# Transposes deferred behind the next scores in a hybrid attention trunk, and one key tile written in place of copied

## The chip, the cores and the metric

One core of a Trainium2 chip runs the whole program. The metric is the device time of one execution in microseconds (us), the median of several; lower is better. The engines that matter here are PE (TensorE, matmuls and transposes), DVE (VectorE), ACT (ScalarE), POOL (GpSimd) and the DMA queues.

## What is computed

Two layers over x (512 tokens, 1024 wide, float32). Each layer normalizes x, projects it with one matrix of 4096 columns, runs two groups of attention heads on the result, gates both, and projects back:

```python
h = rmsnorm(x, norm_g[l]);  proj = h @ w_in[l]
out_a = neighborhood_attention(q_a, k_a, v_a, na_rpb[l])        # group A: 8 heads x 64
p = softmax(q_b k_b^T / 8 + t5_bias)                            # group B: 4 heads, two maps each
out_b = rmsnorm((p[:, 0] - lam * p[:, 1]) @ v_b, subln_g[l]) * (1 - lam_init)
y = concat([out_a * silu(g_a), out_b * silu(g_b)]);  x = x + y @ w_out[l]
```

A last RMSNorm closes the trunk.

## The kernel before

Every float32 matmul is made of three (or two) passes on operands that are split into a high and a low part: ACT casts the value to the high part, DVE subtracts that from the value and writes the low part. `split` (L178) does this for a PSUM tile.

Each layer's projection is cut into 16 units of 256 columns (`ORDER`, L32): VB/VA are values, QB/QA queries and keys, GB/GA gates. A unit is a stream of single matmuls: `proj_fm` (L225) yields a 24-pass group of 512 columns, `proj_tm` (L239) a 24-pass group of 256. The generator `flow` (L578) strings the units together, and `fill(ns)` (L580) pulls matmuls worth `ns` nominal nanoseconds out of it (230 for a wide one, 118 for a narrow one). So projection matmuls are poured, as filling, between the steps of attention. When a 24-pass group is complete its evacuation is issued at that very place in the program: `evac_q` and `evac_k` (two pairs of an ACT cast and a DVE subtraction each), `evac_gate` (ACT tanh, DVE `u`), or `split` for values. `W.piece()` (L129) issues one piece of the weight splitting (`hi` on ACT, L116; `lo` on DVE, L121).

No scheduler reorders any of this: `pinned` chains every engine's instructions in the order in which the Python code issues them. Each engine therefore works off its own fixed list.

Group B (`attn_b`, L290) has 4 tiles of 128 queries per head. A tile: 4 score matmuls (L344); per map a DVE bias-and-minimum (L347) and an ACT exponential (L350); DVE reciprocal, ACT scaling (L356), DVE combination `e` (L358); some 26 filling matmuls; then 4 transposes of `e` on PE (L369) and their `split` (`pth` on ACT L179, `ptl` on DVE L180). After tile 1 and tile 3 a pair is complete, and `weigh` (12 matmuls with the values, L300) is put on the list `late`, which the next tile runs 1400 nominal ns behind its scores. After the second pair `close` prepares the head's norm, and `head_norm` goes on the list `later`: a matmul, DVE `row` (L320), three small POOL steps with DMAs between them, and POOL's product with `rb` (L329). `rb` and the gate's `u` (L280) share two buffers.

Group A (`attn_a`, L375) has the same shape with 8 heads as its steps: 8 score matmuls (L386), 4 minimum/exponential steps, a normalization, some 35 filling matmuls, 8 transposes (L414), and `weigh` (8 matmuls into the one `pv` bank, L421) in the next head.

`evac_k` (L263) writes keys into partitions 0 to 63 of `kt` and then has a DMA (L273) copy them to partitions 64 to 127, since the score matmul needs them twice. At each layer's start the scores of head 0 wait for QB0's keys.

Of the kernel before, what the change touches and what calls it, by code (L numbers as in the profile page):

```python
# [9 lines left out]
F32 = mybir.dt.float32  # L10
# [21 lines left out]
ORDER = ("VB0", "QB0", "QB1", "VB1", "QB2", "GB0", "QB3", "VA0", "QA0", "GB1",  # L32
         "QA1", "VA1", "QA2", "QA3", "GA0", "GA1")
FILL_B = 5400
FILL_A = 7800
A_TILES = ((0, 1), (1, 1), (2, 1), (0, 3))
A_PV = ((1, 128, 128, 0, 128), (3, 640, 256, 256, 128), (0, 0, 768, 0, 384), (2, 384, 128, 128, 128))
NA_BLOCKS = ((0, (0, 1, 2, 3)), (1, (0, 1, 2, 3)), (3, (2, 3, 0, 1)))
# [9 lines left out]
def hybrid_encoder(ctx: ExitStack, tc: tile.TileContext, x, norm_g, w_in, na_rpb,  # L48
# [211 lines left out]
            res.append(q)  # L260
        return res

    def evac_k(pp, natural):  # L263
        kt = qk.tile([P, 4, S], F32R, name="kt", bufs=2)
        for m in range(2):
            src = pp[64 * m:64 * m + 64, :]
            kh, kl = kt[0:64, m, :], kt[0:64, 2 + m, :]
            if natural:
                src = src.rearrange("p (b r c) -> p b r c", r=ROWS, c=C8)
                kh, kl = (z.rearrange("p (r b c) -> p b r c", r=ROWS, c=C8) for z in (kh, kl))  # L270
            A.copy(out=kh, in_=src)
            V.tensor_tensor(out=kl, in0=src, in1=kh.bitcast(F32), op=ALU.subtract)  # L272
        soon.append(lambda: A.dma_start(out=kt[64:128].bitcast(F32), in_=kt[0:64].bitcast(F32)))  # L273
        return [(kt[:, m, :], kt[:, 2 + m, :]) for m in range(2)]

    def evac_gate(pp):
# [3 lines left out]
        V.scalar_tensor_tensor(out=u, in0=th, scalar=1.0, in1=pp, op0=ALU.add, op1=ALU.mult)  # L280
        return u

    late, later = [], []

    def run(jobs):
        while jobs:
            jobs.pop(0)()


    def attn_b(h, q, k, vt, yb, nlam, sg, yout, fill, finished):  # L290
        pair = {}

        def weigh(qp):
            if qp == 0:
                pair["pv"] = ps_v.tile([P, S], F32, name="pv")
            pv, (ph, pl) = pair["pv"], pair[qp]
            n = 0
            for kt in range(4):
                for vs, pp in ((0, ph), (0, pl), (1, ph)):
                    T.matmul(out=pv[:, qp * 256:(qp + 1) * 256], lhsT=vt[:, kt, h % 2, vs, :], rhs=pp[:, kt, :],  # L300
                             start=(n == 0), stop=(n == 11))
                    n += 1
            if qp == 1:
                close(pv)

        def close(pv):
            sq, su = (work.tile([64, S], F32, name=nm, tag="s2", bufs=3) for nm in ("sq", "su"))
            A.activation(out=sq, in_=pv[0:64], func=AF.Square)
            A.activation(out=su, in_=pv[64:P], func=AF.Square)
            V.tensor_tensor(out=sq, in0=sq, in1=su, op=ALU.add)  # L310
            A.activation(out=yout, in_=pv, func=AF.Copy, scale=sg)
            sr = work.tile([P, S], F32R, name="sr", tag="s2", bufs=3)
            A.copy(out=sr[0:64], in_=sq)
            V.tensor_tensor(out=sr[64:P], in0=sq, in1=sr[0:64].bitcast(F32), op=ALU.subtract)
            later.append(lambda: head_norm(pv, sr))

        def head_norm(pv, sr):
            T.matmul(out=pv[0:2, :], lhsT=ones_r, rhs=sr, start=True, stop=True)
            row = work.tile([1, S], F32, name="row", tag="th", bufs=2)
            V.tensor_scalar(out=row, in0=pv[0:1, :], scalar1=1.0 / P, scalar2=1e-5, op0=ALU.mult, op1=ALU.add)  # L320
            ms = small.tile([P, 4], F32, name="ms")
            nc.gpsimd.dma_start(out=ms, in_=row.rearrange("o (p a) -> o p a", a=4))  # L322
            rs = small.tile([P, 4], F32, name="rsb")
            G.tensor_tensor(out=rs, in0=ms, in1=nhalf, op=ALU.pow)
            rs_d = dram.tile([1, S], F32, name="rs_d", bufs=2)
            nc.gpsimd.dma_start(out=rs_d.rearrange("o (p a) -> (o p) a", a=4), in_=rs)
            rb = work.tile([P, S], F32, name="rb", tag="u", bufs=2)
            nc.gpsimd.dma_start(out=rb, in_=rs_d.broadcast_to([P, S]))
            G.tensor_tensor(out=yout, in0=yout, in1=rb, op=ALU.mult)  # L329
            finished()  # L330

        for qt in range(4):
            qp, qi = divmod(qt, 2)
            if qi == 0:
                pair[qp] = [w4.tile([P, 4, 256], F32R, name=nm, tag="w4k") for nm in ("pth", "ptl")]
            e = w4.tile([P, 2, S], F32, name="w4k")
            mn = small.tile([P, 2], F32, name="mn")
            z = small.tile([P, 2], F32, name="z")
            sts = []
            for m in range(2):  # L340
                st = ps_s.tile([P, S], F32, name="st")
                sts.append(st)
                for i in range(2):
                    T.matmul(out=st, lhsT=q[m][:, qt * P:(qt + 1) * P], rhs=k[m][i], start=(i == 0), stop=(i == 1))  # L344
            for m, st in enumerate(sts):
                lt = work.tile([P, S], F32, name="lt", bufs=2)
                V.tensor_tensor_reduce(out=lt, in0=st, in1=yb[:, 48 - 16 * qt:560 - 16 * qt],  # L347
                                       scale=-1.0, scalar=3e38, op0=ALU.add, op1=ALU.min,
                                       accum_out=mn[:, m:m + 1])
                A.activation(out=e[:, m, :].rearrange("p (b r c) -> p b r c", r=ROWS, c=C8),  # L350
                             in_=lt.rearrange("p (r b c) -> p b r c", r=ROWS, c=C8),
                             func=AF.Exp, bias=mn[:, m:m + 1], scale=-1.0, accum_out=z[:, m:m + 1])
            W.piece()
            rz = small.tile([P, 2], F32, name="rz")
            V.reciprocal(out=rz, in_=z)
            A.activation(out=e[:, 0, :], in_=e[:, 0, :], func=AF.Copy, scale=rz[:, 0:1])  # L356
            V.tensor_scalar_mul(rz[:, 1:2], rz[:, 1:2], nlam)
            V.scalar_tensor_tensor(out=e[:, 0, :], in0=e[:, 1, :], scalar=rz[:, 1:2], in1=e[:, 0, :],  # L358
                                   op0=ALU.mult, op1=ALU.add)
            fill(700)  # L360
            run(later)
            W.piece()
            fill(700)
            run(late)
            W.piece()
            fill(FILL_B - 1400)
            pt = ps_t.tile([P, 4, P], F32, name="pt")
            for kt in range(4):
                T.transpose(out=pt[:, kt, :], in_=e[:, 0, kt * P:(kt + 1) * P], identity=ident)  # L369
            split(pt, *(z[:, :, qi * P:(qi + 1) * P] for z in pair[qp]))  # L370
            if qi == 1:
                late.append(lambda qp=qp: weigh(qp))


    def attn_a(hd, half, q, k, vt, ba, s_out, fill, finished):  # L375
        ptt = [w4.tile([P, 8, P], F32R, name=nm, tag="w4k") for nm in ("pth", "ptl")]
        z = small.tile([P, 4], F32, name="za")
        mn = small.tile([P, 4], F32, name="mna")
        rz = small.tile([P, 4], F32, name="rza")
# [8 lines left out]
                         start=(i == 0), stop=(i == 1))  # L388
        for j in range(4):
            st = sts[j // 2][:, (j % 2) * 256:(j % 2) * 256 + 256]  # L390
            e = work.tile([P, 256], F32, name="ea", bufs=4)
            es.append(e)
            i0 = (0, 4, 4, 8)[j]
            V.tensor_tensor_reduce(out=e, in0=st, in1=ba[:, 64 * i0:64 * i0 + 256],  # L394
                                   scale=-1.0, scalar=3e38, op0=ALU.add, op1=ALU.min, accum_out=mn[:, j:j + 1])
            A.activation(out=e, in_=e, func=AF.Exp, bias=mn[:, j:j + 1], scale=-1.0, accum_out=z[:, j:j + 1])  # L396
        W.piece()
        for j in range(0, 4, 2):
            V.reciprocal(out=rz[:, j:j + 2], in_=z[:, j:j + 2])
            V.tensor_scalar_mul(es[j], es[j], rz[:, j:j + 1])  # L400
            A.activation(out=es[j + 1], in_=es[j + 1], func=AF.Copy, scale=rz[:, j + 1:j + 2])
        fill(900)
        run(later)
        W.piece()
        fill(1000)
        run(late)
        W.piece()
        fill((FILL_A - 1900) // 2)
        W.piece()
        fill((FILL_A - 1900) // 2)  # L410
        for g in range(2):
            pt = ps_t.tile([P, 4, P], F32, name="pt")
            for i in range(4):
                T.transpose(out=pt[:, i, :], in_=es[2 * g + i // 2][:, (i % 2) * P:(i % 2 + 1) * P], identity=ident)  # L414
            split(pt, *(z[:, 4 * g:4 * g + 4, :] for z in ptt))

        def weigh():
            pv = ps_v.tile([P, S], F32, name="pv")
# [9 lines left out]
            V.scalar_tensor_tensor(out=s_out[lo:lo + 64], in0=pv[lo:lo + 64], scalar=0.5, in1=tmp[lo:lo + 64],  # L428
                                   op0=ALU.mult, op1=ALU.add)
            finished()  # L430

        late.append(weigh)


    seq = []
# [96 lines left out]
    for l in range(DEPTH):  # L532
# [19 lines left out]
        def unit(u):  # L552
# [11 lines left out]
            elif kind in ("QB", "QA"):  # L564
                qq = []
                yield from proj_fm(w, 0, 64, lambda pp: qq.extend(evac_q(pp)))
                nat = kind == "QB"
                yield from proj_fm(w, P, 64 if nat else 0, lambda pp: qks.update({u: (qq, evac_k(pp, nat))}))
            else:
                c = 2 * i + (4 if kind == "GB" else 0)  # L570
                for m in range(2):
# [54 lines left out]
                   b, ys[p], fill, lambda p=p: finished(p, 2))  # L626
        fill(1 << 30)
        run(later)

        last = l == DEPTH - 1  # L630
        xt = [None] * NB
# [175 lines left out]
```

## Time and profile before

| | |
|---|---|
| three runs | 631.48, 631.99, 633.75 us (median 631.99) |
| profiled execution | 630.65 us, span 628.9 us from first to last instruction |
| mean granted TensorE clock | 0.985 of full |
| PE busy | 589.3 us, 94% of the span |
| DVE busy | 401.4 us, 64% |
| ACT busy | 354.6 us, 56% |
| POOL busy | 74.3 us, 12% |
| group B of layer 0, layer 1 | 46.7 to 183.6 us, 351.5 to 483.2 us |

The busy shares are means over stages. What a stage is worth is read from the waits of PE in it, and from which instruction on another engine ended each of them. Matmuls overlap in the pipeline, so the times between starts tell more than the durations of single ones.

### The profile page before, as it was taken

Reading aid. Unit: us, or ns where it says so; the run is one execution under the profiler, and the core shown is the slowest. Engines: PE = TensorE matmul, PEld = TensorE weight load, DVE = VectorE, ACT = ScalarE, POOL = GpSimd, SP = SyncE. Lnnn points to the kernel's source line nnn. Section 1 sums busy time; section 2 is a strip of 40 time slices with the busy share of each in tenths; the row PEclk is TensorE's granted clock in tenths of the full one; section 3 lists DMA queues with packets and bytes.
Section 4 is the critical chain, followed back from the end, with each engine's and each line's share of the span. In section 5 each row is a group of like instructions: output and inputs, shape, how many; then the busy total and the mean of one; then the engine's idle time right before and its main releaser. Section 6 shows DMA issues by size and latency. Waiting matters only on the chain.

```text
span 628.9 us, 8843 instructions
## 1 busy us (share of the span) xinstructions
PE 589.3 (94%) x3230; PEld 502.5 (80%) x3230; DVE 401.4 (64%) x883; ACT 354.6 (56%) x782; POOL 74.3 (12%) x91
## 2 busy tenths in 40 slices
PE   8979999899987999989999999999999799998995
PEld 7858987788767888878898798878887688887883
DVE  4555675677757577785564667577675657875662
ACT  6435564756548476774243467566664746775331
POOL 5300003011110300110000000211111030001100
PEclk9999999999999999999999999999999989997999
DMA  7743224233325253346415432413332524533523
GB/s 267 136 120 100 86 76 109 87 77 116 85 70 166 80 156 117 111 150 223 178 72 181 120 101 85 117 53 102 109 100 70 166 77 125 152 125 102 194 74 100
DMA packets 25165, 74.47 MB, mean 118 GB/s; under 512 B 7329, under 2 KB 7329, under 8 KB 24098
## 3 DMA queue, kind: packets, MB, share of 16 engines
q1 hardware_dynamic: 22368, 63.12, 29.6%
q10 hardware_dynamic: 1282, 8.39, 6.3%
q0 software_dynamic: 1472, 2.40, 3.0%
q8 instruction: 25, 0.41, 0.3%
q14 instruction: 18, 0.15, 0.1%
HBM read 60.23 MB, written 4.21 MB: 102 GB/s over the span
## 4 chain that ended last, share of the span: by engine, by line
PE 42%; DVE 12%; ACT 10%; issue 4%; DMA 3%; POOL 1%; ACTq 0%; POOLq 0%; DVEq 0%
PE pp L232 16%; PE pp L652 12%; PE pp L245 5%; ACT w4k L350 2%; DVE ptl L180 2%; PE pv L421 2%; DVE wl L121 2%; PE pt L414 2%; PE pv L652 2%; DMA rb<-rs_d 2%; ACT ea L396 1%; DVE kt L272 1%; ACT wh L116 1%; PE st L386 1%; DVE qs L258 1%
## 5 line engine op out<-in xcount | busy, mean ns | idle before, releaser
L121 DVE TENSOR_TENSOR wl<-wraw,wh 128x512 fp32r<-128x512 f32 x148 | 102.3, 707 | 17.0 <-ACT wh L116 16.5
L232 PE MATMUL pp<-hTl,wh 128*128 128x512 f32 x384 | 100.5, 395 | 0.0
L116 ACT CAST wh<-wraw 128x512 fp32r<-128x512 f32 x148 | 87.2, 611 | 23.2 <-DMA wraw<-in_w_in_dram 9.9
L232 PE MATMUL pp<-hTh,wh 128*128 128x512 f32 x384 | 100.2, 396 | 0.0
L232 PE MATMUL pp<-hTh,wl 128*128 128x512 f32 x384 | 99.9, 395 | 0.0
L232 PEld LDWEIGHTS pp<-hTl,wh 128*128 128x128 f32 x384 | 71.6, 188 | 16.1 <-issue 0.2
L232 PEld LDWEIGHTS pp<-hTh,wh 128*128 128x128 f32 x384 | 71.7, 190 | 16.0 <-ACT wh L116 0.4
L232 PEld LDWEIGHTS pp<-hTh,wl 128*128 128x128 f32 x384 | 71.5, 188 | 16.0 <-issue 0.3
L350 ACT ACTIVATE w4k<-lt,mn 128x512 f32<-128x512 f32 x64 | 45.8, 717 | 65.3 <-DVE mn L347 65.3
L245 PE MATMUL pp<-wh,hTh 128*128 128x256 f32 x224 | 64.4, 287 | 0.7 <-DVE v L180 0.4
L245 PE MATMUL pp<-wl,hTh 128*128 128x256 f32 x224 | 64.1, 286 | 0.3 <-DVE wl L121 0.3
L245 PE MATMUL pp<-wh,hTl 128*128 128x256 f32 x224 | 64.1, 286 | 0.0
L180 DVE TENSOR_TENSOR ptl<-pt,pth 128x512 fp32r<-128x512 f32 x64 | 42.5, 685 | 18.3 <-ACT pth L179 17.7
L179 ACT CAST pth<-pt 128x512 fp32r<-128x512 f32 x64 | 36.1, 589 | 30.0 <-PE pt L369 17.6
L245 PEld LDWEIGHTS pp<-wh,hTh 128*128 128x128 f32 x224 | 43.2, 193 | 1.9 <-DVE v L180 0.7
L396 ACT ACTIVATE ea<-ea,mna 128x256 f32<-128x256 f32 x64 | 31.8, 498 | 22.8 <-DVE mna L394 22.8
L245 PEld LDWEIGHTS pp<-wl,hTh 128*128 128x128 f32 x224 | 43.1, 192 | 1.3 <-DVE wl L121 0.5
L344 PE MATMUL st<-kt,qs 128*128 128x512 f32 x128 | 38.3, 422 | 5.6 <-DMA kt<-kt 5.6
L245 PEld LDWEIGHTS pp<-wh,hTl 128*128 128x128 f32 x224 | 43.2, 193 | 0.3
L347 DVE CUSTOM_DVE_ANT_0 lt<-st,yb 128x512 f32<-128x512 f32 x64 | 41.4, 682 | 2.6 <-PE st L344 2.6
L358 DVE SCALAR_TENSOR_TENSOR w4k<-w4k,rz 128x512 f32<-128x512 f32 x32 | 25.2, 787 | 22.9 <-ACT w4k L356 22.9
L322 POOL DMA_DIRECT2D ms<-row x8 | 4.6, 575 | 283.5 <-DVE row L320 283.5
(123 smaller groups left out, 1028.5 us busy)
## 6 DMA issues: line engine op xcount, KB each, us to landing
wraw<-in_w_in_dram SPq DMA_DIRECT2D x64, 512.0 KB, 3.4
kt<-kt ACTq DMA_DIRECT2D x16, 512.0 KB, 4.2
wraw<-in_w_out_dram SPq DMA_DIRECT2D x16, 512.0 KB, 3.3
ba<-in_na_rpb_dram SPq DMA_DIRECT2D x16, 384.0 KB, 4.0
y<-in_x_dram SPq DMA_DIRECT2D x8, 512.0 KB, 5.6
yb<-in_t_table_dram SPq DMA_DIRECT2D x8, 280.0 KB, 3.6
rb<-rs_d POOLq DMA_DIRECT2D x8, 256.0 KB, 4.5
xs_d<-y SPq DMA_DIRECT2D x4, 512.0 KB, 3.1
```

The costliest lines, as they stand in the source:

```text
L116: A.copy(out=wh[:, 2 * i:2 * i + 2, :], in_=r[:, 2 * (i % 2):2 * (i % 2) + 2, :])
L121: V.tensor_tensor(out=wl[:, ks, :], in0=r[:, 2 * (i % 2):2 * (i % 2) + 2, :], in1=wh[:, ks, :].bitcast(F32), op=ALU.subtract)
L179: A.copy(out=oh, in_=ps)
L180: V.tensor_tensor(out=ol, in0=ps, in1=oh.bitcast(F32), op=ALU.subtract)
L232: T.matmul(out=pp, lhsT=a[:, kc, cs], rhs=b[:, kc, c0:c0 + S], start=(n == 0), stop=(n == 3 * KC - 1))
L245: T.matmul(out=pp[:, 0:256], lhsT=a[kc][:, c0:c0 + P], rhs=b[:, kc, :], start=(n == 0), stop=(n == 3 * KC - 1))
L344: T.matmul(out=st, lhsT=q[m][:, qt * P:(qt + 1) * P], rhs=k[m][i], start=(i == 0), stop=(i == 1))
L347: V.tensor_tensor_reduce(out=lt, in0=st, in1=yb[:, 48 - 16 * qt:560 - 16 * qt], scale=-1.0, scalar=3e38, op0=ALU.add, op1=ALU.min, accum_o ...
L350: A.activation(out=e[:, m, :].rearrange("p (b r c) -> p b r c", r=ROWS, c=C8), in_=lt.rearrange("p (r b c) -> p b r c", r=ROWS, c=C8), fun ...
L358: V.scalar_tensor_tensor(out=e[:, 0, :], in0=e[:, 1, :], scalar=rz[:, 1:2], in1=e[:, 0, :], op0=ALU.mult, op1=ALU.add)
L396: A.activation(out=e, in_=e, func=AF.Exp, bias=mn[:, j:j + 1], scale=-1.0, accum_out=z[:, j:j + 1])
L652: T.matmul(out=pp, lhsT=a[k // 2][:, k % 2, t * P:(t + 1) * P], rhs=b[:, kc, :], start=(half + kc + i == 0), stop=(half == 1 and kc == 3 a ...
```

## The change

The transposes and their split move into a function `turn`, which is put on a new list `turns` and run in the following tile or head, 1500 nominal ns of filling behind that one's scores. The softmax's tail (reciprocal, scaling, combination) moves behind that `turn` as well. `later` now runs ahead of both, and `late` (the value matmuls) 3300 nominal ns behind the scores in group B and 4100 in group A; since `turn` is what puts `weigh` on `late`, the two fall into the same tile. Group A's nominal filling per head drops from 7800 to 7200. QB0's keys are written to both halves by ACT and DVE (4 pairs in place of 2 and a DMA). Group A's `e` moves to one tile of the `w4k` pool.

```diff
-FILL_A = 7800
+FILL_A = 7200
@@ evac_k
-    def evac_k(pp, natural):
+    def evac_k(pp, natural, direct=False):
...
+            for p0 in (0, 64) if direct else (0,):
+                kh, kl = kt[p0:p0 + 64, m, :], kt[p0:p0 + 64, 2 + m, :]
...
+                A.copy(out=kh, in_=src)
+                V.tensor_tensor(out=kl, in0=src, in1=kh.bitcast(F32), op=ALU.subtract)
+        if not direct:
+            soon.append(lambda: A.dma_start(out=kt[64:128].bitcast(F32), in_=kt[0:64].bitcast(F32)))
@@ attn_b, behind the exponentials
+            fill(700)
+            run(later)
             W.piece()
+            fill(800)
+            run(turns)
             rz = small.tile([P, 2], F32, name="rz")
...
-            fill(700)
-            run(later)
             W.piece()
-            fill(700)
+            fill(1800)
             run(late)
             W.piece()
-            fill(FILL_B - 1400)
-            pt = ps_t.tile([P, 4, P], F32, name="pt")
...
+            fill(FILL_B - 3300)
+            def turn(e=e, qp=qp, qi=qi):
+                pt = ps_t.tile([P, 4, P], F32, name="pt")
+                for kt in range(4):
+                    T.transpose(out=pt[:, kt, :], in_=e[:, 0, kt * P:(kt + 1) * P], identity=ident)
+                split(pt, *(z[:, :, qi * P:(qi + 1) * P] for z in pair[qp]))
+                if qi == 1:
+                    late.append(lambda: weigh(qp))
+            turns.append(turn)
@@ unit
-                yield from proj_fm(w, P, 64 if nat else 0, lambda pp: qks.update({u: (qq, evac_k(pp, nat))}))
+                yield from proj_fm(w, P, 64 if nat else 0, lambda pp: qks.update({u: (qq, evac_k(pp, nat, u == "QB0"))}))
```

`attn_a` is changed in the same way (fills of 700, 800, 2600 and twice 1550 nominal ns).

What this does to the engines' lists is shown at three places. First PE in layer 0 at group B's head 1, tile 0, a tile with value matmuls (`pt` are the transposes, `st` the scores, `pp` the filling, `pv<-pth` the first value matmul). Before:

```order
L369 MATMUL pt<-ident,w4k 128x128 x4
L344 MATMUL st<-kt,qs 128x512 x4
L232 MATMUL pp<-hTh,wh 128x512 x7
L232 MATMUL pp<-hTl,wh 128x512
L300 MATMUL pv<-pth,v 128x256
L300 MATMUL pv<-ptl,v 128x256
```

and now:

```order
L347 MATMUL st<-kt,qs 128x512 x4
L232 MATMUL pp<-hTh,wh 128x512 x5
L232 MATMUL pp<-hTl,wh 128x512 x3
L376 MATMUL pt<-ident,w4k 128x128 x4
L232 MATMUL pp<-hTl,wh 128x512 x5
L232 MATMUL pp<-hTh,wl 128x512 x3
L303 MATMUL pv<-pth,v 128x256
L303 MATMUL pv<-ptl,v 128x256
```

The transposes went from ahead of the scores to 8 filling matmuls behind them, and the value matmuls from 8 to 16 filling matmuls behind the scores.

Second DVE at the same tile (`qs` the queries' evacuation, `lt,mn` the two minimum steps, `wl` a weight piece, `ptl` the split's subtraction). Before:

```order
L258 SCALAR_TENSOR_TENSOR qs<-pp,qs 64x512 x2
L180 TENSOR_TENSOR ptl<-pt,pth 128x4x128
L347 ISA lt,mn<-st,yb 128x512
L347 ISA mn 128x1
L347 ISA lt,mn<-st,yb 128x512
L347 ISA mn 128x1
L121 TENSOR_TENSOR wl<-wraw,wh 128x512
L355 RECIPROCAL rz<-z 128x2
```

and now:

```order
L258 SCALAR_TENSOR_TENSOR qs<-pp,qs 64x512 x2
L350 ISA lt,mn<-st,yb 128x512
L350 ISA mn 128x1
L350 ISA lt,mn<-st,yb 128x512
L350 ISA mn 128x1
L121 TENSOR_TENSOR wl<-wraw,wh 128x512
L180 TENSOR_TENSOR ptl<-pt,pth 128x4x128
L362 RECIPROCAL rz<-z 128x2
```

The subtraction `ptl` now stands behind the new tile's minimum steps. Its cast on ACT stands behind the two exponentials and, where there is one, a weight cast:

```order
L257 ACTIVATE qs<-pp 64x512 x2
L353 ACTIVATE w4k,z<-lt,mn 128x512 x2
L116 CAST wh<-wraw 128x512
L179 CAST pth<-pt 128x4x128
L363 ACTIVATE w4k<-w4k,rz 128x512
```

Third DVE at head 3, tiles 1 and 2 of layer 0, as it stands now (`row` belongs to head 2's norm, `u` to the two gates of unit GB1):

```order
L323 TENSOR_SCALAR row<-pv 1x512
L121 TENSOR_TENSOR wl<-wraw,wh 128x512
L283 SCALAR_TENSOR_TENSOR u<-th,pp 128x512
L180 TENSOR_TENSOR ptl<-pt,pth 128x4x128
...
L350 ISA mn 128x1
L121 TENSOR_TENSOR wl<-wraw,wh 128x512
L283 SCALAR_TENSOR_TENSOR u<-th,pp 128x512
L180 TENSOR_TENSOR ptl<-pt,pth 128x4x128
L362 RECIPROCAL rz<-z 128x2
```

Before, `row` stood behind its tile's combination (L358); now it stands directly behind the minimum steps. The second `u` stands ahead of the `ptl` that the value matmuls of that very tile read; before, these read a `ptl` that stood a tile earlier.

## Rows read from the trace of the kernel before

**Rows 1.** The waits of PE: line, what ended them, us in total, times, longest.

```profile
PE pt L369 <- DVE w4k L358: 9.0, 9, 2.4
PE pv L421 <- ACT ea L401: 7.4, 2, 4.6
PE st L344 <- DMA kt<-kt: 5.6, 2, 4.6
...
PE pv L300 <- DVE ptl L180: 1.6, 5, 0.4
```

**Rows 2.** Timeline, layer 0's first scores: start us, us, engine, line, [idle before <- releaser].

```profile
38.20 2.02 PE L232 MATMUL pp<-hTl,wh 128*128 128x512 f32 x8
39.44 0.69 DVE L272 TENSOR_TENSOR kt<-pp,kt 64x512 fp32r<-64x512 f32 x1 [0.65 <-ACT kt L271]
40.06 2.02 PE L232 MATMUL pp<-hTh,wl 128*128 128x512 f32 x8
40.16 0.51 ACTq L273 DMA_DIRECT2D kt<-kt  x1
46.73 2.04 PE L344 MATMUL st<-kt,qs 128*128 128x512 f32 x4 [4.64 <-DMA kt<-kt]
48.57 2.50 PE L232 MATMUL pp<-hTh,wh 128*128 128x512 f32 x8
```

**Rows 3.** Timeline, layer 0, head 1 tile 0.

```profile
77.92 0.60 PE L369 MATMUL pt<-ident,w4k 128*128 128x128 f32 x4
78.28 1.17 PE L344 MATMUL st<-kt,qs 128*128 128x512 f32 x4
80.59 0.69 DVE L180 TENSOR_TENSOR ptl<-pt,pth 128x512 fp32r<-128x512 f32 x1
81.19 0.68 DVE L347 CUSTOM_DVE_ANT_0 lt<-st,yb 128x512 f32<-128x512 f32 x1
81.33 0.39 PE L300 MATMUL pv<-ptl,v 128*128 128x256 f32 x1
81.92 0.72 ACT L350 ACTIVATE w4k<-lt,mn 128x512 f32<-128x512 f32 x1 [1.48 <-DVE mn L347]
83.35 0.60 ACT L116 CAST wh<-wraw 128x512 fp32r<-128x512 f32 x1
83.86 0.72 ACT L356 ACTIVATE w4k<-w4k,rz 128x512 f32<-128x512 f32 x1
```

**Rows 4.** Timeline: scores and subtraction at the earliest and latest of 16 such places.

```profile
62.75 1.17 PE L344 MATMUL st<-kt,qs 128*128 128x512 f32 x4
64.07 0.68 DVE L180 TENSOR_TENSOR ptl<-pt,pth 128x512 fp32r<-128x512 f32 x1
...
483.22 1.19 PE L386 MATMUL st<-kt,qs 128*128 128x256 f32 x8
486.10 0.69 DVE L180 TENSOR_TENSOR ptl<-pt,pth 128x512 fp32r<-128x512 f32 x1
```

**Rows 5.** Timeline, layer 0, head 3: two tiles' scores, head 2's row, the second gate.

```profile
156.73 1.17 PE L344 MATMUL st<-kt,qs 128*128 128x512 f32 x4
159.45 0.69 DVE L180 TENSOR_TENSOR ptl<-pt,pth 128x512 fp32r<-128x512 f32 x1
164.14 0.67 DVE L320 TENSOR_SCALAR row<-pv 1x512 f32<-1x512 f32 x1
164.75 1.17 PE L344 MATMUL st<-kt,qs 128*128 128x512 f32 x4
177.72 0.69 DVE L280 SCALAR_TENSOR_TENSOR u<-th,pp 128x512 f32<-128x512 f32 x1 [5.83 <-POOL y L329]
```

**Rows 6.** Group A's first value matmuls (layer 0), and the gated window around layer 1's.

```profile
202.53 0.35 PE L421 MATMUL pv<-pth,v 128*128 128x256 f32 x1 [2.74 <-ACT ea L401]
...
500.00:510.00 10.00, 5.89 (x32) 5.62 (x33) 5.89 (x19) 5.14 (x15) 2.21 (x3) 0.83 0.51 180
```

The columns of the window are its length, the busy us of PE, PE's weight loads, DVE, ACT and POOL with their instructions, the granted clock, the DMA share and GB/s.

More of the change, by code (lines that the diff above doesn't have):

```diff
@@ L266, in evac_k @@
             src = pp[64 * m:64 * m + 64, :]
-            kh, kl = kt[0:64, m, :], kt[0:64, 2 + m, :]
             if natural:
                 src = src.rearrange("p (b r c) -> p b r c", r=ROWS, c=C8)
[L270 to L273, printed above, removed]
+            for p0 in (0, 64) if direct else (0,):
+                kh, kl = kt[p0:p0 + 64, m, :], kt[p0:p0 + 64, 2 + m, :]
+                if natural:
+                    kh, kl = (z.rearrange("p (r b c) -> p b r c", r=ROWS, c=C8) for z in (kh, kl))
+                A.copy(out=kh, in_=src)
+                V.tensor_tensor(out=kl, in0=src, in1=kh.bitcast(F32), op=ALU.subtract)
+        if not direct:
+            soon.append(lambda: A.dma_start(out=kt[64:128].bitcast(F32), in_=kt[0:64].bitcast(F32)))
         return [(kt[:, m, :], kt[:, 2 + m, :]) for m in range(2)]
@@ L281, in evac_gate @@
         return u
-    late, later = [], []
+    late, later, turns = [], [], []
     def run(jobs):
@@ L359, in attn_b @@
                                    op0=ALU.mult, op1=ALU.add)
-            fill(700)
-            run(later)
             W.piece()
-            fill(700)
+            fill(1800)
             run(late)
             W.piece()
-            fill(FILL_B - 1400)
-            pt = ps_t.tile([P, 4, P], F32, name="pt")
[L368 to L372, printed above, removed]
+            fill(FILL_B - 3300)
[7 more added lines that the diff above has]
+            turns.append(turn)
     def attn_a(hd, half, q, k, vt, ba, s_out, fill, finished):
-        ptt = [w4.tile([P, 8, P], F32R, name=nm, tag="w4k") for nm in ("pth", "ptl")]
+        et = w4.tile([P, 4, 256], F32, name="ea", tag="w4k")
+        ptt = []
         z = small.tile([P, 4], F32, name="za")
@@ L390, in attn_a @@
             st = sts[j // 2][:, (j % 2) * 256:(j % 2) * 256 + 256]
-            e = work.tile([P, 256], F32, name="ea", bufs=4)
+            e = et[:, j, :]
             es.append(e)
@@ L396, in attn_a @@
             A.activation(out=e, in_=e, func=AF.Exp, bias=mn[:, j:j + 1], scale=-1.0, accum_out=z[:, j:j + 1])
+        fill(700)
+        run(later)
         W.piece()
+        fill(800)
+        run(turns)
         for j in range(0, 4, 2):
@@ L401, in attn_a, with turn @@
             A.activation(out=es[j + 1], in_=es[j + 1], func=AF.Copy, scale=rz[:, j + 1:j + 2])
-        fill(900)
-        run(later)
         W.piece()
-        fill(1000)
+        fill(2600)
         run(late)
         W.piece()
-        fill((FILL_A - 1900) // 2)
+        fill((FILL_A - 4100) // 2)
         W.piece()
[L410 to L415, printed above, removed]
+        fill((FILL_A - 4100) // 2)
+        def turn():
+            ptt.extend(w4.tile([P, 8, P], F32R, name=nm, tag="w4k") for nm in ("pth", "ptl"))
+            for g in range(2):
+                pt = ps_t.tile([P, 4, P], F32, name="pt")
+                for i in range(4):
+                    T.transpose(out=pt[:, i, :], in_=es[2 * g + i // 2][:, (i % 2) * P:(i % 2 + 1) * P], identity=ident)
+                split(pt, *(z[:, 4 * g:4 * g + 4, :] for z in ptt))
+            late.append(weigh)
+        turns.append(turn)
         def weigh():
@@ L430, in weigh @@
             finished()
-        late.append(weigh)
     seq = []
@@ L628, in hybrid_encoder @@
         run(later)
+        run(turns)
         last = l == DEPTH - 1
```

## The prediction

> **What bounds the kernel now.** PE does: it is busy through most of the span, and what it still loses stands in the list of its waits, which I read first [rows 1]. Four entries carry the argument. The transposes of group B wait nine times for DVE's combination, 9.0 us. The first value matmuls of group A wait twice for the `pv` bank, 7.4 us. The first scores of a layer wait for the key copy, 5.6 us, and the value matmuls of group B for the subtraction `ptl`, 1.6 us in five small pieces. Then I read the timeline at each place, to see what stands on DVE and ACT around the wait. What the reader is to see there is that DVE runs behind PE: at the 16 places where a group of 12 value matmuls follows a tile's or a head's scores (8 per layer), the subtraction that it needs begins 1.32 us behind the scores' start at the earliest and 2.88 us at the latest [rows 4], in sum 32.8 us over the 16. So PE waits little for `ptl` today only because `ptl` is first in DVE's list there.
>
> The sum below is made against the profiled execution, 630.65 us, and then put on the median of the runs, 631.99, which is 1.3 us above it. No change can be told from one of 0.5%, some 3 us.
>
> **The key copy.** Before, the last of two cast-and-subtract pairs ends at 40.1 us, the copy is issued at 40.16 and the scores begin at 46.73, after 4.64 us of waiting; PE's filling had ended at about 42.1 [rows 2]. A pair takes 0.65 + 0.69 = 1.34 us, since each cast waits for the subtraction before it. Two more pairs end at 42.8, so 0.7 us of waiting stays in layer 0, and nothing of the 1.0 us in layer 1: 5.6 - 0.7 = 4.9 us saved. After the long wait PE also ran slower for a while: the 4 scores took 2.04 us where they take 1.17 elsewhere [rows 2, 3], the next 8 filling matmuls 2.50 instead of 2.02 [rows 2]. That is 1.35 us, and I use it as the price of one drop of the granted clock. Together -6.2 us. The DMA page of the Trainium skill (DMA: Bandwidth & Descriptors, Anatomy of one DMA) fits 2.0 us plus bytes over 436 GB/s for a transfer that POOL issues; by that estimate a 512 KB copy lands in 3.2 us, at 43.4, and the edit would be worth some 0.6 us in layer 0 instead of 3.9. The measured wait decides against it.
>
> **The transposes' waits.** Each transpose now comes a whole tile later than its combination could need, behind the next scores and 8 filling matmuls. All nine waits go: -9.0 us. The 0.36 us of the transposes themselves [rows 3] only change places.
>
> **The value matmuls' waits.** This is what takes their place. In DVE's list `ptl` now stands behind the new tile's two minimum steps, and its cast on ACT behind two exponentials and usually a weight cast. What stood ahead of `ptl` before (evacuations, pieces) now stands ahead of the first minimum step, so that step can begin where `ptl` began. From there: 0.73 us to the first exponential, 1.43 to the weight cast, 0.51 for that, 0.74 from subtraction to the second value matmul [rows 3], and from cast to subtraction 0.65 as in the key pairs [rows 2]: 4.06 us. PE reaches that matmul 3.05 us behind the scores' start before [rows 3], and now 0.36 us (transposes) and 1.86 us (8 more filling matmuls, from 38.20 to 40.06 [rows 2]) later: 5.27. So each place waits for its lag less 1.21 us. The nine waits at the transposes all stood directly ahead of one of the 16 places; without them PE gets there earlier and DVE does not, so they are added: 32.8 + 9.0 - 16 x 1.21 = 22.4 us.
>
> Corrections, each by the order of the lists. Seven of the 16 places have no weight cast (-0.51 each) and four of these another cast instead (+0.4 to +0.6): -1.7. In two, a key evacuation stands ahead of `ptl`, two pairs of 1.34: +5.4. In one per layer (head 3, tile 2) the gate's `u` stands ahead of it, and `u` waits for POOL to release `rb`, 13.6 us behind `row` [rows 5]. `row` moves up to behind the minimum steps, about 2.72 + 1.38 us behind its tile's scores; `u` can start at 17.7, `ptl` ends its service at 19.1, and PE is there at 8.0 + 5.3 = 13.3 [rows 5]: some 5.7 us. I take 5 us, since an earlier wait would delay PE too, and 8.7 beyond what these two places were counted with. Against this, four places owed their large lag (17.0 us with the transposes' waits) to DVE's waits for `u`, which now happen elsewhere; with the mean of the other twelve, 1.8, that is -9.8. So far 25.0 us.
>
> One more cost has no row: with `ptl` between exponentials and reciprocal, DVE's chain per tile grows. The reciprocal could start 2.2 us behind the first minimum step (about when the weight cast starts, 83.35 [rows 3]); now it starts after `ptl`, 3.3 + 0.6 us behind, while the 0.6 us ahead of the step falls away: about +1.1 us per tile. Nothing of it shows if every wait of PE gives DVE time to catch up; if ten of the 16 places pass on one tile's growth, it is 11. Most tiles were late before, but PE's new waits do hand time back: I take 6. Forecast for these waits 31.0, against 1.6 before: +29.4 us. Bounds 11 (rival below) and 36.
>
> **Group A's first value matmuls.** They wait for `row` of the last group B head to free `pv`, and `row` stood behind the whole softmax. Now it stands behind the minimum steps only, and the value matmuls 4100 instead of 1900 nominal ns behind the scores. Gone: -7.4, and two clock drops (in the window around layer 1's the granted clock means 0.83, so part of it ran at 1.2 instead of 2.4 GHz [rows 6]) at 1.35: -10.1 us.
>
> **The rest.** The two 5 us waits are longer than the 2.74 us one [rows 6], behind which the clock fell: +2.7. The clock drops of the other new waits are bounded by 0 and 5 x 1.35; most are nearer to the 2.4 us one at the transposes [rows 1], so 0. The smaller nominal filling moves one matmul per head, none away; the cover is the 24-pass stream, which runs dry in the last head as before. There the value matmuls now follow the transposes with nothing between, but the last transposes' wait for their normalization shrinks by about as much: 0, bounds -2 and +3.
>
> Sum: -6.2 - 9.0 + 29.4 - 10.1 + 2.7 = +6.8, so 638.8 us on the median.
>
> **Rivals.** *DVE catches up* (faster). Each PE wait is idle time in which DVE and ACT work off their lists; if after the first such wait the lag stays under 1.21 us nearly everywhere, the 16 places wait 11 us, almost all at the two gates: 631.99 - 6.2 - 9.0 + 9.4 - 10.1 + 2.7 = 618.8. It decides at that lag. For it: DVE is idle for over a third of the span, and in the mean of twelve places only 0.6 us is missing. Against: the lag was there in the kernel before with PE waiting just as often, and the chain got longer. The Trainium skill (Perfetto Trace Analysis, Optimization Strategy) says to find the gaps on the busiest engine and make what they wait for start sooner or finish faster. By that rule the change gains. 22%.
>
> *Even* (632): the lengthening costs nothing and the gates' waits are half as long, 24 us in all. 13%.
>
> *The clock falls at most new waits* (slower still): waits at the upper bound of 36 us, and seven drops in place of two: -6.2 - 9.0 + 34.4 - 10.1 + 9.5 = +18.6, so 650.6. For it: one 2.74 us wait was enough [rows 6]. Against: the 2.4 us one cost nothing that I see. 15%.
>
> **The numbers.** The forecast holds 50%. Slower by over 0.5% are it and the third rival, 65%; within 0.5% the second, 13%; faster the first, 22%. The range reaches from the first rival's time to just under the third's, 619 to 650; some 2 in 10 lie outside.
>
> **What would show it.** Right: in the waits of PE, no transposes behind the combination, no `kt` DMA at the layer starts, no long wait at the `pv` of group A (now L439), but the value matmuls of group B (now L303) behind `ptl` with 25 to 36 us, the longest at head 3 tile 2, about 5 us each. Wrong: if these stay under 15 us in all, the step that carries DVE's lag over unchanged has failed; if the first scores wait 2 us or more, the key step; if group A's value matmuls still wait over 2 us, the step on `row`.

## The result, and the profile after

The changed kernel takes 662.89 us (median of 4 runs, 659.36 to 664.68) beside 632.87 us for the kernel before on the same chip: a ratio of 1.0467, 95% interval [1.0413, 1.0522]. It is slower by some 30 us. The forecast had been 638.8 us, with a range that ended at 650: the sign was right, the size was not.

The page of the changed kernel, its own span and the rows of engines and clock:

```profile
span 662.9 us, 8884 instructions
...
PE 611.4 (92%) x3230; PEld 518.3 (78%) x3230; DVE 404.2 (61%) x887; ACT 361.0 (54%) x786; POOL 75.8 (11%) x91
...
PEclk9999898999987999989999989899987899998998
```

The span grew by 34.0 us (628.9 to 662.9 in the two profiled executions). PE's busy time grew by 22.1 of these (589.3 to 611.4) with the same 3230 matmuls, its idle time by 11.9 (39.6 to 51.5). So only a third of the loss is waiting. The waits of PE, to be laid beside [rows 1] (line, what ended them, us in total, times, longest):

```profile
PE pv L303 <- ACT pth L179: 16.3, 12, 3.3
PE pv L303 <- DVE ptl L180: 13.4, 15, 4.3
PE pv L439 <- DVE ptl L180: 3.5, 8, 0.6
PE pv L439 <- ACT pth L179: 3.3, 2, 1.7
PE pv L321 <- DVE sr L317: 2.7, 3, 1.4
PE pv L496 <- POOL ident masks.py:199: 1.3, 1, 1.3
PE pt L376 <- DVE w4k L365: 0.9, 1, 0.9
```

The reader is to see three things. The transposes (L376, before L369) went from 9.0 to 0.9 us, and `kt` is gone from the list. The value matmuls of group B (L303, before L300) went from 1.6 to 29.7 us, half of it put down to the cast and half to the subtraction of the same split. And the matmul of the head's norm (L321) now waits for the square root `sr`, 2.7 us, which it had not done.

The timeline at one of the 16 places shows how such a wait comes about (start us, us, engine, line, operation; in brackets the idle time before and what ended it):

```profile
98.86 1.10 PE L347 MATMUL st<-kt,qs 128*128 128x512 f32 x4
99.51 0.75 DVE L365 SCALAR_TENSOR_TENSOR w4k<-w4k,rz 128x512 f32<-128x512 f32 x1 [0.60 <-ACT w4k L363]
100.18 1.29 DVE L121 TENSOR_TENSOR wl<-wraw,wh 128x512 fp32r<-128x512 f32 x2
...
101.65 0.60 PE L376 MATMUL pt<-ident,w4k 128*128 128x128 f32 x4
101.99 0.68 DVE L350 CUSTOM_DVE_ANT_0 lt<-st,yb 128x512 f32<-128x512 f32 x1
...
102.71 0.73 ACT L353 ACTIVATE w4k<-lt,mn 128x512 f32<-128x512 f32 x1 [1.71 <-DVE mn L350]
...
103.43 0.71 ACT L353 ACTIVATE w4k<-lt,mn 128x512 f32<-128x512 f32 x1
...
104.14 0.60 ACT L116 CAST wh<-wraw 128x512 fp32r<-128x512 f32 x1
104.65 0.57 ACT L179 CAST pth<-pt 128x512 fp32r<-128x512 f32 x1
105.25 0.69 DVE L180 TENSOR_TENSOR ptl<-pt,pth 128x512 fp32r<-128x512 f32 x1 [1.36 <-ACT pth L179]
105.27 0.39 PE L303 MATMUL pv<-pth,v 128*128 128x256 f32 x1 [1.15 <-ACT pth L179]
...
106.00 0.46 PE L303 MATMUL pv<-ptl,v 128*128 128x256 f32 x1 [0.34 <-DVE ptl L180]
```

PE has the transposes done by 102.3. Their cast starts at 104.65 only, because it stands on ACT behind two exponentials (L353) and a weight cast, and the exponentials behind minimum steps that DVE reaches 3.1 us after the scores. DVE, itself late, then idles 1.36 us for that cast. The same shows in DVE's list of waits: first the kernel before, then the changed one.

```profile
DVE ptl L180 <- ACT pth L179: 17.7, 9, 4.4
```

```profile
DVE ptl L180 <- ACT pth L179: 48.3, 32, 2.2
DVE u L283 <- POOL y L332: 14.1, 4, 5.1
```

The gate's `u` still waits for POOL to release `rb`, 14.1 us in four waits.

Most of the other two thirds stands in the windows of 5 us (their length, PE's busy us with its matmuls, the granted clock, the DMA share, GB/s). Changed kernel:

```profile
65.00:70.00 5.00, 2.22 (x12) 0.86 0.31 105
70.00:75.00 5.00, 5.00 (x29) 0.80 0.34 105
...
105.00:110.00 5.00, 4.39 (x17) 0.66 0.42 86
...
180.00:185.00 5.00, 2.32 (x11) 0.63 0.18 74
185.00:190.00 5.00, 5.00 (x18) 0.69 0.00 0
```

A window at 0.66 has lost 0.34 x 5 = 1.7 us of full clock, that is, part of it was granted 1.2 instead of 2.4 GHz. Summed over the windows between the first scores and 620 us, the kernel before lost 8.5 us at 4 places (1.7 at three of them, 3.4 at one), and the changed one 23.8 us at 11 places (eight times 1.7, and three times twice that behind the waits of 3.27, 4.07 and 4.35 us). The length of the wait doesn't set the loss, though: in the kernel before the waits of 4.64 and 4.63 us lost 1.7 each, and the one of 1.89 us lost the 3.4. Part of it fell while PE was waiting anyway. With windows of 0.25 us, each weighted by PE's busy share in it, the loss is 7.7 us before and 21.5 after, 13.8 more; this is the better estimate of what the clock cost. By the whole span's mean clock the unweighted loss is nearly the same: (1 - 0.985) x 628.9 = 9.4 us against (1 - 0.961) x 662.9 = 25.9.

Every one of the 11 places stands at a wait of value matmuls (in three the clock falls before the wait has ended), and the groups of matmuls show it. L300 and L303 are the same 192 instructions, before and after (line, operation, count; busy us, mean ns; idle before and its releasers):

```profile
L300 PE MATMUL pv<-pth,v 128*128 128x256 f32 x128 | 25.8, 282 | 0.0
...
L300 PE MATMUL pv<-ptl,v 128*128 128x256 f32 x64 | 18.9, 295 | 1.6 <-DVE ptl L180 1.6
```

```profile
L303 PE MATMUL pv<-pth,v 128*128 128x256 f32 x128 | 35.7, 356 | 16.5 <-ACT pth L179 16.3
...
L303 PE MATMUL pv<-ptl,v 128*128 128x256 f32 x64 | 24.2, 378 | 13.6 <-DVE ptl L180 13.4
```

They take 15.2 us more of busy time (59.9 against 44.7; durations of neighbours overlap, so this is not a sum on the path). That leaves some 7 us of the 22.1. About 2.7 are the start: in the changed kernel the filling ahead of the first scores ran until 44.83, in the one before until about 42.1. The difference arises in PE's first 14 us, where four matmuls of 256 columns took 1.15 us (at 12.97) in place of 0.75 (at 10.41), with a granted clock of 1.00 shown for both. The start varies so from run to run: the first scores began between 42.1 and 44.8 us in the nine others, which all share the key edit. The rest I can't place.

### The profile page after: what moved, and what is told of

It is laid out like the page before. It is cut to its first block, busy times and chain, and to the rows that moved or that the text cites. A ratio compares the mean times of both kernels' runs of the same rounds, so it can differ in the third digit from the quotient of the medians.

```text
span 662.9 us, 8884 instructions
## 1 busy us (share of the span) xinstructions
PE 611.4 (92%) x3230; PEld 518.3 (78%) x3230; DVE 404.2 (61%) x887; ACT 361.0 (54%) x786; POOL 75.8 (11%) x91
## 5 line engine op out<-in xcount | busy, mean ns | idle before, releaser
L121 DVE TENSOR_TENSOR wl<-wraw,wh 128x512 fp32r<-128x512 f32 x148 | 104.5, 719 | 14.9 <-ACT wh L116 14.4
L232 PE MATMUL pp<-hTl,wh 128*128 128x512 f32 x384 | 104.5, 404 | 0.0
L232 PE MATMUL pp<-hTh,wh 128*128 128x512 f32 x384 | 103.5, 401 | 0.0
L232 PE MATMUL pp<-hTh,wl 128*128 128x512 f32 x384 | 103.4, 399 | 0.0
L232 PEld LDWEIGHTS pp<-hTh,wl 128*128 128x128 f32 x384 | 71.4, 191 | 14.8 <-issue 0.2
L353 ACT ACTIVATE w4k<-lt,mn 128x512 f32<-128x512 f32 x64 | 45.8, 717 | 64.5 <-DVE mn L350 64.5
L180 DVE TENSOR_TENSOR ptl<-pt,pth 128x512 fp32r<-128x512 f32 x64 | 42.9, 688 | 48.8 <-ACT pth L179 48.3
L303 PE MATMUL pv<-pth,v 128*128 128x256 f32 x128 | 35.7, 356 | 16.5 <-ACT pth L179 16.3
L303 PEld LDWEIGHTS pv<-pth,v 128*128 128x128 f32 x128 | 27.7, 252 | 21.3 <-ACT pth L179 21.2
L363 ACT ACTIVATE w4k<-w4k,rz 128x512 f32<-128x512 f32 x32 | 23.1, 723 | 37.5 <-DVE rz L362 35.2
```

Of the source, the lines that this page charges most:

```text
L121: V.tensor_tensor(out=wl[:, ks, :], in0=r[:, 2 * (i % 2):2 * (i % 2) + 2, :], in1=wh[:, ks, :].bitcast(F32), op=ALU.subtract)
L180: V.tensor_tensor(out=ol, in0=ps, in1=oh.bitcast(F32), op=ALU.subtract)
L232: T.matmul(out=pp, lhsT=a[:, kc, cs], rhs=b[:, kc, c0:c0 + S], start=(n == 0), stop=(n == 3 * KC - 1))
```

## The experiments

The theory after the result: the time is lost because the split of a transposed tile stands behind the next tile's softmax in ACT's and DVE's lists, and because PE's new waits cost clock besides their own length. The rivals: it is PE's place of the transposes that costs; or the waits alone cost and the clock is only a sign of them.

| kernel | us | ratio to before, 95% interval |
|---|---|---|
| the change | 662.89 | 1.0467 [1.0413, 1.0522] |
| 1: keys only | 628.85 | 0.9945 [0.9917, 0.9972] |
| 2: transposes early on PE | 654.86 | 1.0372 [1.0333, 1.0411] |
| 3: split early in the lists | 624.05 | 0.9899 [0.9832, 0.9966] |
| 4: waits filled | 651.25 | 1.0316 [1.0272, 1.0361] |
| 5: norm row moved up | 624.75 | 0.9883 [0.9830, 0.9935] |
| 6: values early | 632.41 | 1.0000 [0.9970, 1.0030] |
| 7: change, third buffer | 648.11 | 1.0243 [1.0183, 1.0303] |
| 8: 5 with third buffer | 616.75 | 0.9764 [0.9704, 0.9823] |
| 9: 3 with third buffer | 617.52 | 0.9752 [0.9691, 0.9813] |

### 1. The kernel before, with the key edit alone

```diff
-                yield from proj_fm(..., evac_k(pp, nat))
+                yield from proj_fm(..., evac_k(pp, nat, u == "QB0"))
```

with the new `evac_k`, and nothing else.

> The kernel before, with only QB0's keys written to both halves in place of the copy. Theory (the key step of the prediction): PE's 5.6 us of waiting for the copy becomes under 1 us and one drop of the granted clock goes, so 5 to 7 us faster, 626 to 628 us. Rival (the four serial pairs cost as much as the copy, or the wait only moves to the next transposes): within 2 us of before.

Measured: 0.9945, 3.5 us by the ratio, less than the 5 to 7 expected. The 5.6 us of waiting for `kt` are gone, but the transposes behind them wait more:

```profile
PE pt L372 <- DVE w4k L361: 10.3, 12, 1.6
PE pv L424 <- ACT ea L404: 7.4, 2, 4.6
```

Twelve waits with 10.3 us in place of nine with 9.0 [rows 1]. Part of what PE saves at a layer's start it pays again later, since DVE's work behind it isn't any earlier; that reason is argued and not tested. Nor did the clock give anything back: summed as above it lost 8.5 us, as before. The drop behind the key wait is gone, but another stands at 265 to 275 us. This run's start was about 2.4 us later than the one of [rows 2] without its wait, which hides some more of the gain in the profile.

### 2. The change, with the transposes early on PE

```diff
+            W.piece()
+            run(turns)
             fill(700)
             run(later)
-            W.piece()
             fill(800)
-            run(turns)
```

`turn` is issued behind the exponentials, and so directly behind the scores on PE. On ACT and DVE its split still stands behind the exponentials and minimum steps. The norm's `row` now comes behind the split. `attn_a` likewise.

> The changed kernel with the transposes of a tile or head issued directly behind the next one's scores on PE, 8 filling matmuls earlier, while cast and subtraction stay behind the exponentials and minimum steps on ACT and DVE; only the evacuations that fell into those 8 matmuls, and the head norm's row, are no longer ahead of them. Theory A (the place in ACT's and DVE's lists makes the value matmuls wait): the waits shrink only at the places where a key or gate evacuation stood ahead, by 10 to 13 us of 30; the rest stays, 15 to 20 us, and the time is about 645 us. Rival B (the transposes come too late on PE): the waits nearly go, under 5 us, and the time is 632 or less.

Measured: 654.86 us, some 8 us better than the change (6 by the ratios, each against the kernel before on its own chip), 23 worse than before and 10 above the 645 expected. The waits moved back to the transposes, and grew there:

```profile
PE pt L376 <- DVE w4k L365: 13.5, 10, 4.0
PE pv L303 <- ACT pth L179: 6.8, 11, 0.9
PE pv L439 <- ACT pth L179: 5.8, 4, 2.4
PE pv L303 <- DVE ptl L180: 4.4, 13, 0.3
```

So PE's place for the transposes was not what cost most.

### 3. The change, with the split early in the lists too

```diff
                     T.matmul(out=st, lhsT=q[m][:, qt * P:(qt + 1) * P], rhs=k[m][i], start=(i == 0), stop=(i == 1))
+            run(turns)
             for m, st in enumerate(sts):
...
             fill(800)
-            run(turns)
```

PE's transposes stand where they do in experiment 2, directly behind the scores. But the split now stands ahead of the minimum steps and the exponentials, and `row` ahead of the normalization as in the change.

> Same PE order as the run with early transposes, but cast and subtraction also stand ahead of the new tile's minimum steps and exponentials on DVE and ACT, as in the kernel before. Theory A: value matmuls of group B wait under 3 us in all, transposes 2 us (their 9.0 less the 1 us of scores that now covers each), group A's value matmuls for pv under 2 us; with the keys' 6 us the time is 612 to 620 us. Rival B (the place on PE decides): like the run with early transposes within 5 us. Rival C (the new DVE order of row and reciprocal costs by itself): 630 or more.

Measured: 624.05 us, above what was expected and still 31 us below experiment 2; the intervals are far apart. The waits at L303 are gone from the list, and DVE waits for the cast 18.1 us in place of 67.1. PE's first entries:

```profile
PE pt L376 <- DVE w4k L365: 7.3, 7, 2.2
PE pt L429 <- DVE rza L413: 6.8, 2, 3.4
PE pv L321 <- DVE sr L317: 6.5, 5, 2.4
```

This settles where the harm is: with PE's transposes at the same place, the place of the split on ACT and DVE (and of `row` and a weight piece, which moved with it) is worth some 30 us. The wait at L321, for the head's norm, grew from 1.4 us in experiment 2 to 6.5.

### 4. The change, with its waits filled by matmuls

```diff
             pv, (ph, pl) = pair["pv"], pair[qp]
+            for i in range(12):
+                T.matmul(out=pv[:, qp * 256:(qp + 1) * 256], lhsT=hTh[:, i % KC, 64:64 + P], rhs=hTh[:, i % KC, 64:320],
+                         start=True, stop=True)
             n = 0
```

Ahead of each of the 16 groups PE gets 12 matmuls whose result the group overwrites: 192 more, work that nobody needs.

> The changed kernel with 12 matmuls of 256 columns, whose result is overwritten, ahead of each of the 16 groups of value matmuls of group B: about 1.4 us of work for PE in place of idle waiting. Theory (the second half of the loss is the granted clock, which falls after waits of 1.2 to 2.5 us): idle time of PE falls by about 20 us, its granted clock rises from 0.961 to about 0.98, and the time FALLS by 6 to 12 us although PE does 23 us more work. Rival (the clock is not what the waits cost): the same or up to 6 us slower.

Measured: 651.25 us, 11.6 less than the change (9.5 by the ratios, with intervals that don't overlap), as the clock theory expected. Such a piece took 1.42 us (from 101.58 to 103.00 at the place shown above, where the group then ran from 103.00 to 105.05), so 16 of them are 22.7 us. The page's row of engines:

```profile
PE 617.3 (95%) x3422; PEld 530.0 (81%) x3422; DVE 404.9 (62%) x887; ACT 360.8 (55%) x786; POOL 75.9 (12%) x91
```

The window that had been at 0.66 is at full clock:

```profile
105.00:110.00 5.00, 5.00 (x24) 1.00 0.46 136
```

The sum closes: PE's idle time fell from 51.5 to 34.1 us (-17.4), the added matmuls cost 22.7, and the other busy time fell from 611.4 to 617.3 - 22.7 = 594.6 (-16.8); together -11.5. Summed as above, its windows lose 8.5 us of clock at 5 places where the change lost 23.8 at 11; weighted by PE's busy share it is 8.4 against 21.5, so the clock accounts for 13.0 of the 16.8. Less waiting and added filling alone would have made it 5.3 us slower; the gain is the clock's. That the waits alone cost is refuted. It is a test and no remedy: the kernel stays 20 us behind the one before.

### 5 and 6. The norm's row moved up; the value matmuls moved back

Experiment 5 is experiment 1, so with no deferral, but with `later` run ahead of the normalization (so too in `attn_a`):

```diff
             W.piece()
+            fill(700)
+            run(later)
             rz = small.tile([P, 2], F32, name="rz")
...
-            fill(700)
-            run(later)
```

> The kernel before with QB0's keys written in place, and with the head norm's matmul and row issued ahead of the softmax's normalization in both groups, as the change does, but no transposes deferred. Theory: group A's first value matmuls wait for the row that frees pv, so their 7.4 us become under 2 and the two clock drops behind them go; the gate's u is released some 2 us earlier, so the transposes' 9 to 10 us become about 6. Together 8 to 14 us less than the run with the keys alone: 614 to 621 us. Rival (pv is held by something else, or DVE's lag takes the gain): 626 or more.

Experiment 6 is experiment 3 with the value matmuls 1500 (group B) and 1900 (group A) nominal ns behind the scores and the normalization earlier:

```diff
-            fill(800)
             rz = small.tile([P, 2], F32, name="rz")
...
+            fill(800)
+            run(late)
             W.piece()
             fill(1800)
-            run(late)
```

> The run with cast and subtraction ahead of the minimum steps, and with the value matmuls moved back to some 1500 (group A 1900) nominal ns behind the scores, so that the head norm's preparation gets 1800 nominal ns more. Theory: the 6.5 us that PE waited for the head norm's operand (sr) become under 1.5, value matmuls wait 1 to 2 us for the subtraction, 617 to 622 us. Rival (DVE's list is the bound, so the wait moves to the value matmuls): 624 us as that run, within 2.

Measured: 624.75 us for 5 and 632.41 for 6, both above their ranges. In 5 the `pv` wait of group A halves (7.4 to 3.7 us), and the transposes wait 12.0 instead of 10.3; its interval overlaps that of experiment 1, so the step's own gain, about 4 us, is not firmly measured. Experiment 6 is 8 us slower than experiment 3, with intervals that don't overlap, and level with the kernel before. The wait that it was made for did go (`sr` at L321 from 6.5 to 0.4 us), but the transposes wait 11.5 us in place of 7.3, and the value matmuls of group A 3.9 in place of 1.3 for `row`. So the split's place isn't all that counts: with the split early, the order of the other steps is still worth 8 us, and which of those moved here costs them isn't separated.

### 7, 8 and 9. A third buffer for the gate's `u` and `rb`

```diff
-        u = work.tile([P, S], F32, name="u", bufs=2)
+        u = work.tile([P, S], F32, name="u", bufs=3)
...
-            rb = work.tile([P, S], F32, name="rb", tag="u", bufs=2)
+            rb = work.tile([P, S], F32, name="rb", tag="u", bufs=3)
```

Experiment 7 puts it into the change, 8 into experiment 5 (with group A's `e` in one `w4k` tile, as in the change, to make room), 9 into experiment 3.

> The changed kernel with a third buffer for the gate's u and rb, nothing else. Theory (the two longest waits, head 3 tile 2, are u waiting for POOL's release of rb ahead of the subtraction): DVE's 14.1 us of waiting for POOL at u go to nearly 0, the waits of 4.1 and 4.8 us there become 1 to 2 us, and with the clock drops behind them the time falls by 6 to 12 us, to 650 to 656. Rival (DVE's and ACT's chain is late there anyway): less than 3 us.

> The run with the row ahead of the normalization, with the third buffer for u and rb, and group A's e in the w4k pool as in the change to make room. Theory: DVE no longer waits for POOL, the transposes' waits for the combination fall to 1 to 3 us and no wait of PE in group B is over 1 us: 605 to 614 us. Rival (what is left in group B is DVE's own work): within 3 us of the run without the buffer.

> The deferred transposes with their split at the head of ACT's and DVE's lists, and a third buffer for the gate's u and rb. Theory A (what costs in the change is DVE's chain; the gate's wait for rb is a part of it that the third buffer takes out): DVE's waits for POOL in the gate, 16.1 us in the run with the split at the head of the lists, go, and of PE's waits there (transposes 7.3 and 6.8, head norm 6.5) 4 to 8 us go with them: 616 to 621, near the kernel with the norm row moved up and the same buffer (616.8). Rival B (with the split early DVE has slack, and its waits at the gate cost PE nothing): 622 to 625, as without the buffer.

Measured: 648.11, 616.75 and 617.52 us. Experiment 7 beat its range. In the change the longer waits had looked so (head 3, tile 2 of layer 0):

```profile
181.34 0.69 DVE L283 SCALAR_TENSOR_TENSOR u<-th,pp 128x512 f32<-128x512 f32 x1 [4.52 <-POOL y L332]
...
182.68 0.58 PE L303 MATMUL pv<-ptl,v 128*128 128x256 f32 x1 [4.07 <-DVE ptl L180]
```

Now the wait of `u` for POOL is gone, and the two longest waits of PE with it.

```profile
PE pv L303 <- ACT pth L179: 16.3, 12, 3.3
PE pv L303 <- DVE ptl L180: 5.7, 15, 0.8
```

That is 13.4 - 5.7 = 7.7 us of waiting, yet the time fell by 14.8 (14.2 by the ratios). Of the 17.8 us that the span lost, PE's idle time is 7.1 (51.5 to 44.4), the clock 8.3 (weighted, 21.5 to 13.2), and 2.7 are the start, which was earlier in this run (first scores at 42.08 in place of 44.83). In 9 the gain over 3 is 1.5% of the kernel before, with intervals that don't overlap, and the time lies in the range of the theory of DVE's chain. Of PE's waits 3.5 us went, where that theory had 4 to 8; the 6.8 us at group A's transposes stayed:

```profile
PE pt L429 <- DVE rza L413: 6.8, 2, 3.4
PE pv L321 <- DVE sr L317: 5.3, 5, 1.6
PE pt L376 <- DVE w4k L365: 5.0, 7, 1.6
```

Experiment 8 missed its range of 605 to 614: the transposes still wait 7.8 us where 1 to 3 were expected. It is 8.0 us faster than experiment 5, with intervals that don't overlap. Experiments 8 and 9 are the fastest kernels here, some 15 us below the one before, and can't be told from each other. One has the transposes behind the next scores and one ahead of them, and in neither does the split stand behind a softmax. They differ in other steps too, so that PE's place for the transposes makes no difference is suggested by this and not shown.

## Why the prediction was right in its sign and wrong in its size

**The waits came out as forecast.** For the value matmuls of group B I had 31.0 us; they are 29.7. The longest two were to stand at head 3, tile 2, with about 5 us each; they stand there with 4.07 and 4.35, and experiment 7 shows that they came from `u` waiting for POOL, as argued. The transposes' waits went from 9.0 to 0.9 (forecast 0). The key wait went from 5.6 to none (forecast 0.7 left). Group A's `pv` wait is gone from the first head (experiment 5, with `row` moved alone, only halved it, so that the later place of the value matmuls may have done the rest); L439 holds 4.3 us at the two last heads, in place of the 4.2 at L414 before, and 2.5 us in small pieces. In all PE's waits were to grow by 8.1 us (29.4 - 9.0 - 4.9 - 7.4), and its idle time grew by 11.9. The 2.7 us of the head's norm (L321), a wait that the forecast doesn't have, and these 2.5 more than cover the difference.

That the sum came out doesn't show that each correction in it did. The 6 us for DVE's longer chain per tile were tested by no run alone; experiment 6 made that chain shorter but moved the value matmuls too. One correction has a slip in it: the -9.8 sets four places with 17.0 us, the transposes' waits included, against a mean of 1.8 us without them. With the waits the mean of the other twelve is 2.07, and the correction -8.7. That is 1.1 us, small beside the miss.

**The step that failed is the clock,** in "The rest": "most are nearer to the 2.4 us one at the transposes, so 0". All clock terms of the forecast together were -1.35 - 2.7 + 2.7 = -1.35 us. Measured, it cost 13.8 us more than before (7.7 to 21.5, weighted by PE's busy share; 8.5 to 23.8 unweighted), a miss of 15.1 out of the 24 between the forecast and the result. The number of drops was wrong above all. The forecast had one fewer than before; counted in units of 1.7 us of lost clock there were 14 in place of 5, nine more. The ten that the forecast lacks are 13.5 us at its own price of 1.35. The price was a little low: 21.5 over 14 is 1.5. The clock fell at 11 places in place of 4, behind every wait of the value matmuls of 1.49 us in one place (1.15 + 0.34) or more, and behind none of 0.93 us or less. I had taken the one wait at a transpose that cost no clock as the pattern, though the other row that I had shown, 2.74 us at a value matmul [rows 6], was of the kind that the change makes.

With 13.8 in place of -1.35 the same sum gives 638.8 + 15.1 = 653.9 us. The unforeseen waits (11.9 - 8.1 = 3.8) bring it to 657.7, 1.7 us below the fastest run of the change and 5 below its median; the rest lies in the start and in the busy time that I can't place.

These sizes come from one trace of each kernel. The mean clocks of all runs give less: 0.961 to 0.966 in the four of the change, 0.969 to 0.984 in the 33 later ones of the kernel before, so a growth of some 11 us. How much of that is the start, where the traces of experiments 4 and 8 lose 3.4 us, the runs without a trace don't show. That the clock is the largest part of the miss holds either way.

**The rivals.** The third one, that the clock falls at most new waits, named the mechanism and had 15%; its 650.6 was too low because it had seven drops where there were eleven places with fourteen, though its waits, 36 us, were 6 too high. Among the reasons against it stood "the 2.4 us one cost nothing that I see", which was true and did not carry over. "DVE catches up" fell: the value matmuls waited 29.7 us and not 11, DVE waited more for ACT (48.3 against 17.7 us), not less, and its share of busy time fell from 64% to 61% while PE waited for it. The rule named there, of the Trainium skill (Perfetto Trace Analysis, Optimization Strategy), says to make what the busiest engine waits for start sooner or finish faster. Experiments 2 and 3 agree with it when it is read strictly: the change made PE ask later but made the split start later too, and lost; starting the split sooner at the same place on PE gained some 30 us.

**The keys.** The forecast was -6.2 us; alone the edit gave 3.5 by the ratio [1.8, 5.2]. The waits it removes went as reckoned. But the transposes behind them waited 1.3 us more, and the drop of the clock that was to go came back at another place.

## What to carry to other kernels

When a step is moved, look where its instructions come to stand on every engine's list: deferring the consumer on PE gains nothing if its producers on ACT and DVE move behind a later softmax. Price a new wait of PE at its length and the clock behind it: here 30 us of such waits cost some 14 us more by the trace, and a buffer that took 7.7 us of waiting away gave back some 14 us. Where the trace shows a wait that cost clock and one that didn't, keep both prices in the range.

## What the runs showed of the hardware that I had not expected

Matmuls whose result is thrown away made a kernel some 10 us faster, with 22.7 us of added work (experiment 4). And the length of a wait doesn't say alone whether the clock falls. Kernel before: a transposes' wait at the end of layer 0's group B and one at layer 1's last head in the timeline, and then the windows around these and around layer 0's last head:

```profile
183.24 0.63 PE L369 MATMUL pt<-ident,w4k 128*128 128x128 f32 x4 [2.40 <-DVE w4k L358]
...
572.41 1.82 PE L414 MATMUL pt<-ident,ea 128*128 128x128 f32 x6 [1.89 <-DVE ea L400]
```

```profile
180.00:185.00 5.00, 2.60 (x18) 1.00 0.00 0
185.00:190.00 5.00, 4.71 (x35) 1.00 0.45 167
...
270.00:275.00 5.00, 2.73 (x17) 1.00 0.43 120
...
570.00:575.00 5.00, 3.06 (x15) 0.69 0.56 189
575.00:580.00 5.00, 5.00 (x19) 0.63 0.00 0
```

A wait of 2.40 us left the clock at full speed, and so did one of 2.27 at the transposes of layer 0's last head (window 270 to 275). Behind one of 1.89 us at the same place of layer 1 it fell, and behind 1.49 us in the changed kernel too. Behind a wait of 1.44 us at the head's norm (L321, changed kernel, at 132.02) it stayed. What sorts them these runs don't settle. The Trainium skill (TensorE: Matmul & The Clock Gate, What's actually happening) puts the penalty of the ramp at under 1% of a typical kernel's span. That is a figure for the ramp and not for drops behind waits in mid-kernel; in this kernel, which waits often, these come to 23.8 of 662.9 us, 3.6%.
